# Fourth to seventh product of a Strassen-like down projection summed in PSUM, and a value projection's second weights and transposes moved behind its first units

## The chip, the cores and the metric

One core of one Trainium2 chip. The time is in device microseconds (us) for one execution of the whole kernel; smaller is better. Engines are named as in the profile: PE is TensorE (matmuls), PEld its weight loads, DVE is VectorE, ACT is ScalarE, POOL is GpSimd, SP is SyncE, whose queue issues every DMA here.

## The reference

One decoder layer on a sequence of 1024 tokens with 1024 features, all in float32. Three sub-layers, each with a residual, a gate and a LayerNorm:

```
def swiglu(h, w_gate, w_up, w_down):
    return (jax.nn.silu(h @ w_gate) * (h @ w_up)) @ w_down
...
h = modulate(x, sh1, sc1)
y = swiglu(h, ffn1_w_gate[l], ffn1_w_up[l], ffn1_w_down[l])
x = layer_norm(ALPHA * x + (1 + g1) * (MACARON * y), ln1_g[l], ln1_b[l])
h = modulate(x, sh2, sc2)
y = token_mix(h, w_in[l], b_forget[l], swa_sinks[l], grp_gain[l], w_out[l])
x = layer_norm(ALPHA * x + (1 + g2) * y, ln2_g[l], ln2_b[l])
h = modulate(x, sh3, sc3)
y = swiglu(h, ffn2_w_gate[l], ffn2_w_up[l], ffn2_w_down[l])
x = layer_norm(ALPHA * x + (1 + g3) * (MACARON * y), ln3_g[l], ln3_b[l])
```

The inner width of the two feed-forward parts is 2816. `token_mix` begins with one projection of h; its value columns and forget-gate columns (648 in all) are computed first, as "units" of 128 tokens.

## The kernel before

Every float32 operand is split into a high and a low part (`split`: ACT casts the high part on L102, DVE subtracts it on L103), and each product of two tiles is three matmuls (`mm3`, L106 to L108).

The two down projections, `down(0, ...)` and `down(1, ...)`, use Strassen's scheme in Winograd's form: the 1024x2816 by 2816x1024 product is cut in halves each way and done as seven half-size products instead of eight. A product is 11 steps (`NG`) of 12 matmuls 128x128x512, into four PSUM banks, one for each 128 tokens of the half. `DOWN` gives the order of the products and their operands: A11, A12, A22, S1 to S4 come from memory (`aT`, L412), B11 to B22 are tiles of the down weights (`home`, L383), and T1 to T4 are sums of these, made on DVE in `weight`: T2 costs three sums a step (L393, L395, L396), T1's step makes T3 (L400) and, in the second feed-forward part, multiplies B21 by the gate (L402).

A product's result leaves its banks while the next product runs in other banks (`PBANKS`: "tp tp y y" and "mm mm mm o" by turns). The running sums of the scheme stand in SBUF stashes (`x1`, `x2`, `x3`, `u4`): a first product is copied by ACT (L477), later ones are added by DVE (L479, L481, L483, L485, L486, L495). `add_to` puts a finished quarter of the output into the residual with two DVE instructions (L423, L424). Such work is held in a list `todo` whose entries are taken one by one behind the steps of the following products. For the last quarter the sum goes straight from the banks to the residual (L490 for the first feed-forward part, L491).

`tail` is the number of last steps of the seventh product that run bank by bank, so that the first banks are finished early: 2 in the first down projection, 7 in the second.

Tiles come from rings of slots: `h` (14 slots: weights, stashes, LayerNorm rows, some operands), `w` and `z` (operands), `u` (loads), `t` (sums), and PSUM `mm` 3, `o` 1, `y` 2, `tp` 2. The order on each engine and queue is fixed when the kernel is built, by a planner that takes whatever is ready by its own estimate of times, earlier code first; slots of a ring are handed out in the order of the code.

After the first down projection, the kernel loads and splits the weights of both value projections (`wv_load` twice, 8 tiles each: ACT L740, DVE L741), normalises the second half of the tokens (four norms, `ln_steps`, up to L170), and then runs 16 units: first-half tokens with `wva` (k = 0 to 3) and `wvb`, then second-half tokens with both. A unit is 24 matmuls into one bank of `mm`, evacuated by ACT (L761) and DVE (L762). Behind the first-half units stand the eight "chunks" that transpose the normalised second half (PE L185 into `tp`, ACT L186, then a split):

```
                if hf == 0:
                    if t or pz:
                        steps[3 + t + 4 * pz]()
```

The second down projection is followed by the last LayerNorm (`final_b`): statistics for four token blocks (`ln_stats`, L158 to L165), then for each block the affine steps (L1333 to L1339) and the store of the output (L1341, L1343).

Of the kernel before, what the change touches and what calls it, by code (L numbers as in the profile page):

```python
# [46 lines left out]
def layer_kernel(ctx, tc, xT, x, c, adaT, adab, wg1, wu1, wd1, wqk, wv1, wv2, bf, sinks,  # L47
# [57 lines left out]
    def mm3(o, lh, ll, rh, rl, start, stop):  # L105
        T.matmul(o, lh, rh, start=start, stop=False)  # L106
        T.matmul(o, lh, rl, start=False, stop=False)  # L107
        T.matmul(o, ll, rh, start=False, stop=stop)  # L108
# [46 lines left out]
    def ln_stats(src):  # L155

        s6 = small([P, 2, 6], "bn", 4)
        V.bn_stats(s6[:, 0], src[:, :HT])  # L158
        V.bn_stats(s6[:, 1], src[:, HT:])
        mv = small([P, 2], "mv", 4)  # L160
        V.bn_aggr(mv, s6)
        ve = small([P, 1], "ve", 4)
        V.tensor_scalar(ve, mv[:, 1:2], LN_EPS, None, op0=ALU.add)
        rs = small([P, 1], "rs", 4)
        G.tensor_tensor(rs, ve, nhalf[:, :1], ALU.pow)  # L165
        return mv, rs

    def ln_norm(src):
        mv, rs = ln_stats(src)
        V.tensor_scalar(src, src, mv[:, 0:1], rs, op0=ALU.subtract, op1=ALU.mult)  # L170
# [194 lines left out]
    def down(ai, wd, gate, alpha, load, steps_a, tail=TAIL):  # L365
# [4 lines left out]
        sums = {}  # L370
# [15 lines left out]

        def weight(kind, g):
            if kind in ("B11", "B21", "B22"):
                return home(kind, g)
            if kind == "T2":  # L390
                b12 = home("B12", g)
                b11, b21, b22 = (raw[k, 0, g] for k in ("B11", "B21", "B22"))
                V.tensor_tensor(b11, b12, b11, ALU.subtract)  # L393
                t = st("t", [P, HT])
                V.tensor_tensor(t, b22, b11, ALU.subtract)  # L395
                V.tensor_tensor(b21, t, b21, ALU.subtract)  # L396
                return t
            if kind == "T1":
                b12, b21 = raw["B12", 0, g], raw["B21", 0, g]
                V.tensor_tensor(b12, raw["B22", 0, g], b12, ALU.subtract)  # L400
                if ai:
                    V.tensor_tensor(b21, b21, gate[:, cols[0]], ALU.mult)  # L402
            return raw[{"T1": "B11", "T3": "B12", "T4": "B21"}[kind], 0, g]
# [13 lines left out]
        def stash():  # L417
            return st("h", [P, 4, HT])

        def add_to(xt, k, n, s, eng=V):  # L420

            y = xt[k][:, cols[n]]
            eng.tensor_tensor(s, s, gate[:, cols[n]], ALU.mult)  # L423
            V.scalar_tensor_tensor(y, y, alpha, s, op0=ALU.mult, op1=ALU.add)  # L424
# [16 lines left out]
        xs = []  # L441
        for i in range(7):
            banks = [psum(q) for q in PBANKS[2 if i == 6 and not ai else i % 2].split()]

            def mul(a, w, g, k):
                mm3(banks[k], a[:, 0, k * P:(k + 1) * P], a[:, 1, k * P:(k + 1) * P], w[:, 0], w[:, 1],
                    g == 0, g == NG - 1)

            tl = tail if i == 6 else 1
            for g in range(NG - tl):  # L450
                a, w = get(i, g)
                for k in range(4):
                    mul(a, w, g, k)
                if i in (0, 4) and 2 <= g < 6:
                    if g == 2:
                        xs.append([])
                    xs[-1].append(load(i // 4, g - 2))
                if todo:
                    for f in todo.pop(0):
                        f()  # L460
            aw = [get(i, g) for g in range(NG - tl, NG)]
            if i in (0, 1, 2, 4):
                new = stash()
                if i == 0:
                    x1 = new
                elif i == 1:
                    x2 = new
                elif i == 2:
                    x3 = new
                else:  # L470
                    u4 = new
            for k in range(4):
                for j in range(tl):
                    mul(*aw[j], NG - tl + j, k)
                b = banks[k]
                if i in (0, 2):
                    A.copy(new[:, k], b)  # L477
                elif i in (1, 4):
                    V.tensor_tensor(new[:, k], x1[:, k], b, ALU.add)  # L479
                    if i == 4:  # L480
                        V.tensor_tensor(x3[:, k], x3[:, k], b, ALU.add)  # L481
                elif i == 3:
                    V.tensor_tensor(x1[:, k], x1[:, k], b, ALU.add)  # L483
                elif i == 5:
                    V.tensor_tensor(u4[:, k], u4[:, k], b, ALU.add)  # L485
                    V.tensor_tensor(x1[:, k], x1[:, k], b, ALU.add)  # L486
                else:
                    s = xs[1][k][:, cols[0]]
                    if not ai:
                        V.tensor_tensor(b, b, gate[:, cols[0]], ALU.mult)  # L490
                    V.tensor_tensor(s, s, b, ALU.subtract)  # L491
            if i == 1:
                todo = [[lambda k=k: add_to(xs[0], k, 0, x2[:, k])] for k in range(4)]
# [11 lines left out]
        while todo:  # L505
            for f in todo.pop(0):
                f()
# [172 lines left out]
    def ln_steps(zt, hf, m, dst, split_to, park=None):  # L680

        def norm(k):
            ln_norm(zt[k])
# [37 lines left out]
    def steps1(z):  # L721
# [5 lines left out]
              steps1)  # L727
# [5 lines left out]
    def wv_load(src, ncol):  # L733
        r = []
        for d0, nk in ((0, 3), (3, 3), (6, 2)):
# [7 lines left out]
        return r  # L743
# [552 lines left out]
    def final_a(zt):  # L1296
# [3 lines left out]
        def stats(k):  # L1300
# [3 lines left out]
            s1, s2, nm, ve = (q[:, j:j + 1] for q in [small([P, 2, 6], "bn", 4)[:, 0]] for j in range(4))  # L1304
# [18 lines left out]
    def final_b(zt):  # L1323
# [20 lines left out]
        for k in range(4):  # L1344
            sc[k] = ln_stats(zt[k])
# [3 lines left out]
    final_b(down(1, wd2, gate_load(2), 1.0, load_x2, final_a, 7))  # L1349
# [59 lines left out]
```

## Time and profile before

| | us |
|---|---|
| median of 3 runs | 1815.85 (1813.96 to 1819.73) |
| the profiled execution, whole | 1817.26 |
| its span, first to last instruction | 1815.5 |
| PE busy | 1750.9 |
| DVE busy | 1547.4 |
| ACT busy | 764.8 |
| first down projection, from its first matmul | 447.40 |
| value projection's units | 661.03 to about 731 |
| second down projection, first to last matmul | 1583.02 to 1796.06 |

A row of the view by windows shows, for a stretch of the span, the busy time of each engine with its number of instructions, the granted clock of PE, the share of DMA and the bytes per second. A row of the timeline shows start, duration, engine, line, operation, output and input, and in brackets how long its engine had been idle and what ended that.

### The profile page before, as it was taken

What the parts mean: (1) busy time and instruction counts of PE and PEld (TensorE: products, weight loads), DVE (VectorE), ACT (ScalarE), POOL (GpSimd) and SP (SyncE); (2) the same over time, 40 slices, a digit from 0 to 9 for tenths busy, and PEclk for the clock granted to TensorE, in tenths of its full rate; (3) what the DMA queues carried; (4) which work ended last, traced back from release to release, by engine and by line L of the source; (5) the groups of instructions that cost most, each with busy time, mean ns of one, the idle gap of its engine ahead of it and who ended that gap; (6) DMA issues with size and microseconds to landing.
All of it is one profiled execution on the core that took longest, in us unless ns stands there. A gap on an engine that the chain in (4) does not pass through costs nothing.

```text
span 1815.5 us, 23554 instructions
## 1 busy us (share of the span) xinstructions
PE 1750.9 (96%) x8114; PEld 1439.7 (79%) x8114; DVE 1547.4 (85%) x2806; ACT 764.8 (42%) x1465; POOL 23.0 (1%) x32
## 2 busy tenths in 40 slices
PE   7999999999999989999999989899999999999995
PEld 5788888888888879877777768678888888888884
DVE  7999999999597996378878887998887878879999
ACT  5433333333544342376556641633233333344480
POOL 0000000000000000000000000000000000000000
PEclk9999999999999999999999999999999999999998
DMA  9355555547754335655677862333233232675442
GB/s 364 123 198 179 191 201 185 178 161 275 259 168 146 88 118 196 215 156 169 180 216 215 238 215 87 117 122 128 87 132 101 99 105 87 231 231 165 134 146 81
DMA packets 147048, 303.44 MB, mean 167 GB/s; under 512 B 15385, under 2 KB 29297, under 8 KB 146929
## 3 DMA queue, kind: packets, MB, share of 16 engines
q1 hardware_dynamic: 146928, 301.94, 51.7%
q8 instruction: 64, 1.05, 0.3%
q14 instruction: 56, 0.45, 0.1%
HBM read 224.17 MB, written 77.71 MB: 166 GB/s over the span
## 4 chain that ended last, share of the span: by engine, by line
PE 83%; DVE 10%; ACT 3%; DMA 2%; issue 1%; POOL 0%; SPq 0%; DVEq 0%; ACTq 0%; POOLq 0%
PE y L106 11%; PE y L107 11%; PE y L108 11%; PE mm L108 10%; PE mm L106 10%; PE mm L107 9%; PE o L106 3%; PE o L108 3%; PE o L107 3%; PE tp L108 2%; PE tp L107 2%; PE tp L106 2%; DVE h L103 1%; PE tp L1121 1%; PE o L1125 1%
## 5 line engine op out<-in xcount | busy, mean ns | idle before, releaser
L102 ACT CAST w<-u 128x512 fp32r<-128x512 f32 x303 | 186.5, 622 | 397.5 <-PE y L108 164.0
L106 PE MATMUL y<-h,w 128*128 128x512 f32 x728 | 287.3, 395 | 5.2 <-ACT h L102 2.1
L107 PE MATMUL y<-h,w 128*128 128x512 f32 x728 | 285.7, 392 | 0.0
L108 PE MATMUL y<-h,w 128*128 128x512 f32 x728 | 284.9, 392 | 0.0
L103 DVE TENSOR_TENSOR w<-u,w 128x512 fp32r<-128x512 f32 x303 | 206.9, 688 | 24.0 <-ACT w L102 23.3
L106 PE MATMUL mm<-h,w 128*128 128x512 f32 x528 | 207.1, 393 | 18.5 <-ACT h L102 15.4
L108 PE MATMUL mm<-h,w 128*128 128x512 f32 x528 | 207.1, 393 | 0.4 <-DVE w L103 0.4
L107 PE MATMUL mm<-h,w 128*128 128x512 f32 x528 | 207.1, 393 | 0.3 <-DVE h L103 0.2
L106 PEld LDWEIGHTS y<-h,w 128*128 128x128 f32 x728 | 137.0, 188 | 33.5 <-ACT h L102 2.5
L108 PEld LDWEIGHTS y<-h,w 128*128 128x128 f32 x728 | 136.8, 188 | 26.6
L107 PEld LDWEIGHTS y<-h,w 128*128 128x128 f32 x728 | 136.9, 188 | 25.9 <-DVE h L103 0.2
L102 ACT CAST w<-t 128x512 fp32r<-128x512 f32 x106 | 65.5, 621 | 185.2 <-PE mm L108 68.4
L106 PEld LDWEIGHTS mm<-h,w 128*128 128x128 f32 x528 | 99.9, 189 | 40.7 <-ACT h L102 15.8
L107 PEld LDWEIGHTS mm<-h,w 128*128 128x128 f32 x528 | 100.2, 190 | 22.1 <-DVE h L103 1.5
L108 PEld LDWEIGHTS mm<-h,w 128*128 128x128 f32 x528 | 100.1, 190 | 21.7 <-DVE w L103 1.1
L102 ACT CAST z<-u 128x512 fp32r<-128x512 f32 x88 | 54.5, 622 | 107.2 <-PE y L108 45.2
L103 DVE TENSOR_TENSOR z<-u,z 128x512 fp32r<-128x512 f32 x88 | 60.5, 692 | 37.3 <-ACT z L102 37.3
L103 DVE TENSOR_TENSOR t<-tp,t 128x512 fp32r<-128x512 f32 (+1 forms) x126 | 73.0, 586 | 20.8 <-ACT t L102 19.5
L102 ACT CAST w<-h 128x512 fp32r<-128x512 f32 x111 | 68.1, 616 | 28.8 <-PE o L108 10.5
L102 ACT CAST t<-tp 128x512 fp32r<-128x512 f32 (+1 forms) x126 | 62.1, 501 | 42.1 <-PE tp L1121 41.0
L103 DVE TENSOR_TENSOR w<-h,w 128x512 fp32r<-128x512 f32 x111 | 75.8, 690 | 1.3 <-ACT w L102 1.3
L103 DVE TENSOR_TENSOR w<-t,w 128x512 fp32r<-128x512 f32 x106 | 73.0, 691 | 1.6 <-ACT w L102 1.1
(357 smaller groups left out, 3941.8 us busy)
## 6 DMA issues: line engine op xcount, KB each, us to landing
u<-aT SPq DMA_DIRECT2D x154, 256.0 KB, 2.7
q<-in_adaT SPq DMA_DIRECT2D x56, 512.0 KB, 3.4
u<-in_wg SPq DMA_DIRECT2D x92, 256.0 KB, 3.0
u<-in_wu SPq DMA_DIRECT2D x90, 256.0 KB, 2.8
aT<-z SPq DMA_DIRECT2D x44, 512.0 KB, 3.5
h<-in_wd SPq DMA_DIRECT2D x88, 256.0 KB, 4.7
qkd<-w SPq DMA_DIRECT2D x26, 512.0 KB, 3.6
aT<-b SPq DMA_DIRECT2D x22, 512.0 KB, 4.1
```

Of the source, the lines that this page charges most:

```text
L102: A.copy(hi, src)
L103: V.tensor_tensor(lo, src, hi.bitcast(F32), ALU.subtract)
L106: T.matmul(o, lh, rh, start=start, stop=False)
L107: T.matmul(o, lh, rl, start=False, stop=False)
L108: T.matmul(o, ll, rh, start=False, stop=stop)
L1121: T.transpose(pt[:, tok(i - q0)], sps[i][:, tok(j)], ident)
L1125: T.matmul(po[:, c0:], vt, ph[:, c0:], start=j == 0, stop=False)
```

## The change

The order of the seven products becomes P1 (A11 B11), P2 (A12 B21), S2 T2, S1 T1, S4 B22, S3 T3, A22 T4. The third, fourth and fifth products are added by PE to the banks that hold the first one (no `start`); the seventh is added to the banks of the sixth, with T4's sign turned. DVE's adds out of the banks become ACT copies of the running sum (after the first, third and fourth product into `u`, `u` again and `u4`, and of the sixth into `p7`), and the second quarter goes from the banks straight into `add_to`. The weights B22 and B12 are asked for step by step from the seventh step of the first product on (`coming`, `AHEAD`). The gate of the last quarter is applied on the banks in both down projections, not on B21 in the second. `second` adds the sixth product, puts the fourth quarter into the residual, and begins that half's LayerNorm statistics (`ln_early`); all entries of `todo` are now taken before the last bank is done.

Ahead of the units only `wva` is loaded; `wvb`'s three pieces stand behind units 1 to 3, and the eight chunks stand two by two behind units 5 to 8. The first two units use banks of `y`.

```diff
-    DOWN = (("A11", "B11"), ("A12", "B21"), ("S4", "B22"), ("S2", "T2"), ("S1", "T1"), ("S3", "T3"), ("A22", "T4"))
-    PBANKS = ("tp tp y y", "mm mm mm o", "y y mm mm")
+    DOWN = (("A11", "B11"), ("A12", "B21"), ("S2", "T2"), ("S1", "T1"), ("S4", "B22"), ("S3", "T3"), ("A22", "T4"))
+    PBANKS = {0: "tp tp y y", 1: "mm mm mm o", 5: "mm mm mm o"}
+    AHEAD = 6
...
+    def ln_early(k, src):
+        begun_stats[k] = small([P, 2, 6], "bn2", 4)
+        V.bn_stats(begun_stats[k][:, 1], src[:, HT:])
...
+        coming = [(kind, g) for kind in ("B22", "B12") for g in range(NG)]
...
-                b12 = home("B12", g)
...
-                V.tensor_tensor(b21, t, b21, ALU.subtract)
+                V.tensor_tensor(b21, b21, t, ALU.subtract)
...
-                if ai:
-                    V.tensor_tensor(b21, b21, gate[:, cols[0]], ALU.mult)
...
+                if len(made) >= AHEAD and coming:
+                    home(*coming.pop(0))
                 made.append(operands(*DOWN[j], h, ring(j, h)))
...
+            if i in PBANKS:
+                sets[i in (1, 5)] = [psum(q) for q in PBANKS[i].split()]
+            banks = sets[i in (1, 5, 6)]
+            more = i not in PBANKS
...
-                    g == 0, g == NG - 1)
+                    g == 0 and not more, g == NG - 1, more)
...
                 if i in (0, 2):
-                    A.copy(new[:, k], b)
-                elif i in (1, 4):
-                    V.tensor_tensor(new[:, k], x1[:, k], b, ALU.add)
-                    if i == 4:
-                        V.tensor_tensor(x3[:, k], x3[:, k], b, ALU.add)
+                    A.copy(u[:, k], b)
+                elif i == 1:
+                    V.tensor_tensor(c[:, k], u[:, k], b, ALU.add)
                 elif i == 3:
-                    V.tensor_tensor(x1[:, k], x1[:, k], b, ALU.add)
+                    A.copy(u4[:, k], b)
                 elif i == 5:
-                    V.tensor_tensor(u4[:, k], u4[:, k], b, ALU.add)
-                    V.tensor_tensor(x1[:, k], x1[:, k], b, ALU.add)
-                else:
+                    A.copy(p7[:, k], b)
+                elif i == 6:
+                    for _ in range(3):
+                        pop()
                     s = xs[1][k][:, cols[0]]
-                    if not ai:
-                        V.tensor_tensor(b, b, gate[:, cols[0]], ALU.mult)
-                    V.tensor_tensor(s, s, b, ALU.subtract)
+                    V.tensor_tensor(b, b, gate[:, cols[0]], ALU.mult)
+                    V.tensor_tensor(s, s, b, ALU.add)
...
-            elif i == 3:
-                todo = [[lambda k=k: V.tensor_tensor(x3[:, k], x3[:, k], x1[:, k], ALU.add)] for k in range(4)]
             elif i == 4:
-                todo = [[lambda k=k: add_to(xs[0], k, 1, x3[:, k])] for k in range(4)] + steps_a(xs[0])
+                todo = [[lambda k=k, b=banks[k]: add_to(xs[0], k, 1, c[:, k], b)] for k in range(4)] + steps_a(xs[0])
             elif i == 5:
-                z = [[lambda k=k, n=n: add_to(xs[1], k, n, (x1, u4)[n][:, k], V)] for n in range(2) for k in range(4)]
+                def second(k):
+                    V.tensor_tensor(u4[:, k], u4[:, k], p7[:, k], ALU.add)
+                    add_to(xs[1], k, 1, u4[:, k])
+                    if early:
+                        early(k, xs[1][k])
+                z = [[lambda k=k: second(k)] for k in range(4)]
+                z += [[lambda k=k: add_to(xs[1], k, 0, u[:, k])] for k in range(4)]
...
-    wva = wv_load(wv1, NV1)
-    wvb = wv_load(wv2, NV2)
+    wva, load_a = wv_load(wv1, NV1)
+    wvb, load_b = wv_load(wv2, NV2)
+    run_all(load_a)
     steps = ln_steps(xb, 1, mod2, t_tile, h2_split(1))
     run_all(steps[:4])
+    between = [[f] for f in load_b] + [[]] + [steps[4 + 2 * k:6 + 2 * k] for k in range(4)]
...
-                p = psum("mm")
+                p = psum("y" if hf + pz == 0 and k < 2 else "mm")
...
-                    if t or pz:
-                        steps[3 + t + 4 * pz]()
-                    if t == 3 and pz:
-                        steps[11]()
+                    run_all(between.pop(0))
```

More of the change, by code (lines that the diff above doesn't have):

```diff
@@ L103, in split, with mm3 @@
         V.tensor_tensor(lo, src, hi.bitcast(F32), ALU.subtract)
[L105 to L108, printed above, removed]
+    def mm3(o, lh, ll, rh, rl, start, stop, more=False):
+        T.matmul(o, lh, rh, start=start, stop=False, skip_group_check=more)
+        T.matmul(o, lh, rl, start=False, stop=False, skip_group_check=more)
+        T.matmul(o, ll, rh, start=False, stop=stop, skip_group_check=more)
     def halves(t):
@@ L369, in down @@
         mixed = {}
-        sums = {}
         def home(kind, g):
@@ L441, in down, with pop @@
         xs = []
+        sets = {}
+        def pop():
+            if todo:
+                for f in todo.pop(0):
+                    f()
         for i in range(7):
-            banks = [psum(q) for q in PBANKS[2 if i == 6 and not ai else i % 2].split()]
+            if i in PBANKS:
+                sets[i in (1, 5)] = [psum(q) for q in PBANKS[i].split()]
+            banks = sets[i in (1, 5, 6)]
+            more = i not in PBANKS
             def mul(a, w, g, k):
                 mm3(banks[k], a[:, 0, k * P:(k + 1) * P], a[:, 1, k * P:(k + 1) * P], w[:, 0], w[:, 1],
-                    g == 0, g == NG - 1)
+                    g == 0 and not more, g == NG - 1, more)
             tl = tail if i == 6 else 1
@@ L505, in down @@
         while todo:
-            for f in todo.pop(0):
-                f()
+            pop()
         return xs[1]
```

68 lines of the change are left out of this document (33 added, 35 removed).

## The prediction

> **What bounds the kernel now.** I read the page first (shares and chain), then the products of the second down projection as windows, then the gap after the first one, then the end.
>
> ```profile
> span 1815.5 us, 23554 instructions
> ...
> PE 1750.9 (96%) x8114; PEld 1439.7 (79%) x8114; DVE 1547.4 (85%) x2806; ACT 764.8 (42%) x1465; POOL 23.0 (1%) x32
> ...
> PE 83%; DVE 10%; ACT 3%; DMA 2%; issue 1%; POOL 0%; SPq 0%; DVEq 0%; ACTq 0%; POOLq 0%
> ```
>
> TensorE ends most of the chain. Fewer VectorE instructions pay only where PE waits. The windows of the second down projection, one for each product, and a last one for what follows PE:
>
> ```profile
> 1583.02:1614.21 31.19, 30.22 (x134) 24.70 (x132) 28.74 (x42) 14.43 (x25) 0.00 (x0) 1.00 0.78 263
> 1614.21:1644.13 29.92, 29.92 (x134) 24.78 (x132) 15.41 (x25) 13.16 (x24) 0.00 (x0) 1.00 0.57 174
> 1644.13:1674.05 29.92, 29.92 (x134) 24.77 (x132) 29.92 (x51) 14.24 (x25) 0.00 (x0) 1.00 0.54 161
> 1674.05:1703.97 29.92, 29.92 (x134) 24.78 (x132) 29.92 (x50) 12.82 (x23) 0.00 (x0) 1.00 0.54 164
> 1703.97:1734.21 30.24, 30.23 (x134) 24.70 (x132) 29.53 (x44) 13.95 (x25) 0.00 (x0) 1.00 0.41 123
> 1734.21:1764.13 29.92, 29.92 (x134) 24.78 (x132) 27.84 (x58) 26.36 (x48) 3.19 (x4) 1.00 0.50 148
> 1764.13:1796.06 31.93, 30.44 (x133) 24.47 (x131) 31.73 (x53) 7.25 (x14) 0.00 (x0) 1.00 0.22 75
> 1796.06:1815.50 19.44, 0.00 (x1) 0.00 (x0) 15.91 (x36) 2.44 (x3) 2.93 (x4) 0.61 0.26 108
> ```
>
> The first column after the bounds is the length, then PE, PEld, DVE, ACT. A product takes 29.92 us with PE never idle, although DVE (29.92 of 29.92) is full in the third and fourth. So most of the 20 DVE instructions that the first down projection loses, and the 27 of the second, lie under PE and give nothing by themselves. Lost are 1.3 us in the first product, 0.3 in the fifth, 2.0 in the seventh, and 19.44 us behind PE's end in which DVE works 15.91.
>
> The other place is the start of the units, in windows of 5 us:
>
> ```profile
> 660.00:665.00 5.00, 5.00 (x34) 4.80 (x33) 5.00 (x11) 0.27 (x1) 0.00 (x0) 1.00 0.31 89
> 665.00:670.00 5.00, 5.00 (x36) 5.00 (x36) 3.99 (x9) 3.29 (x7) 0.00 (x0) 1.00 0.72 229
> 670.00:675.00 5.00, 2.16 (x14) 1.68 (x13) 4.58 (x12) 2.25 (x6) 1.07 (x2) 1.00 0.88 274
> 675.00:680.00 5.00, 2.25 (x9) 1.83 (x10) 4.48 (x11) 0.00 (x0) 1.12 (x3) 0.72 0.36 127
> 680.00:685.00 5.00, 5.00 (x24) 4.95 (x23) 4.25 (x7) 2.06 (x3) 0.00 (x0) 0.60 0.59 183
> 685.00:690.00 5.00, 5.00 (x37) 4.99 (x36) 4.37 (x7) 2.03 (x4) 0.00 (x0) 1.00 0.44 161
> ```
>
> Three windows hold 14 + 9 + 24 = 47 PE instructions where 36 each would be 108. The 61 missing ones are 61 x 5/36 = 8.5 us: 5.6 us of waits (next fence), the rest mostly the granted clock at 0.72 and 0.60.
>
> **The change, step by step.**
>
> *The units.* The first matmul of a unit, PE's waits (total, times, longest) and DVE in the same stretch:
>
> ```profile
> 661.03 0.30 PE L106 MATMUL mm<-h,h 128*128 128x320 f32 x1
> ```
>
> ```profile
> PE tp L185 <- DVE z L170: 5.6, 3, 2.9
> ```
>
> ```profile
> 668.27 1.87 DVE L741 TENSOR_TENSOR h<-u,h 128x328 fp32r<-128x328 f32 x4 [1.01 <-ACT h L740]
> ...
> 673.10 0.50 DVE L741 TENSOR_TENSOR h<-u,h 128x328 fp32r<-128x328 f32 x1 [0.35 <-ACT h L740]
> ...
> 678.17 0.44 DVE L762 TENSOR_TENSOR w<-mm,w 128x320 fp32r<-128x320 f32 x1
> ...
> 679.40 0.81 DVE L170 TENSOR_SCALAR z<-z,s_mv,s_rs 128x1024 f32<-128x1024 f32 x1 [0.33 <-POOL s_rs L165]
> ```
>
> The transposes stand in PE's order behind three units and wait for the norms (L170, the fourth at 679.40); DVE has `wvb`'s splits among the norms, and the first evacuation (L762) comes only at 678.17, so the three `mm` banks are full too. After: five units find a bank (two `y`, three `mm`), and the transposes stand behind the fifth. A unit is 24 x 5/36 = 3.3 to 3.5 us, so the fifth starts at about 675 and the transposes come at about 678.5. DVE's norms lose `wvb`'s 8 splits (1.87/4 = 0.47 each, 3.7 us) and four statistics of 0.6 (2.4 us), so the fourth norm is done near 680.2 - 6.1 = 674. `wvb` is needed from 675 to 678; its last split was at 673.10, and its loads wait for the same slots of `u` as before. Margins of 2 to 5 us: 8.5 us go, between 4 (one of the waits comes back) and 8.5. I take 7.5.
>
> *The end.* Six rows of the timeline, DVE, PE, POOL and SP:
>
> ```profile
> 1788.56 1.31 DVE L423 TENSOR_TENSOR h<-h,b 128x512 f32<-128x512 f32 x2
> ...
> 1795.57 0.68 DVE L424 SCALAR_TENSOR_TENSOR z<-z,h 128x512 f32<-128x512 f32 x1
> ...
> 1810.56 1.41 DVE L1339 SCALAR_TENSOR_TENSOR z<-z,s_rs,h 128x512 f32<-128x512 f32 x2
> ```
>
> ```profile
> 1795.67 0.39 PE L108 MATMUL y<-h 128*128 128x512 f32 x1
> ```
>
> ```profile
> 1798.92 0.55 POOL L165 TENSOR_TENSOR s_rs<-s_ve,nhalf 128x1 f32<-128x1 f32 x1 [39.92 <-DVE s_ve L163]
> ```
>
> ```profile
> 1811.33 0.99 SPq L1341 DMA_DIRECT2D out<-z x2
> ```
>
> The last quarter's `add_to` runs from 1788.56 to 1795.57, the statistics and affine steps to 1811.97, and 3.5 us more pass to the span's end. The easy reading is that eight `add_to` and four statistics leave the tail. But DVE is full throughout (27.84, 31.73 and 15.91 us in the last three windows), so moving work ahead of PE's end only pushes other work behind it. What counts is how much DVE has left to do from 1734 on. In 29.92 us it does 50 or 51 instructions, 0.60 us each. From 1734 the change takes away the rest of the fifth product's adds (3 still to come) and the sixth's 8, and adds 4 in `second` and 4 gates: 3 fewer, 1.8 us. The 24 fewer before 1734 (14.4 us) leave DVE idle in the fourth and fifth products, which it can use only to split ahead, as far as slots go: from about 1.5 steps of lead to about 4, 5 instructions, 3.0 us. The lead now is read from the splits of the sixth product's first and third step, against PE's start of it at 1734.21:
>
> ```profile
> 1729.12 0.71 DVE L103 TENSOR_TENSOR h<-u,h 128x512 fp32r<-128x512 f32 x1
> ...
> 1737.73 0.69 DVE L103 TENSOR_TENSOR h<-u,h 128x512 fp32r<-128x512 f32 x1
> ```
>
> Together 4.8 us. The bounds: 1.8 (no lead), and everything done but the last block's chain: gate, add, one statistics (0.6 each), POOL's 0.55 with small steps (1.3), four affine steps (2.7) and 0.3 of latency make 6.1 us behind PE, where now DVE ends 1811.97 - 1796.06 = 15.9 behind: 9.8 us.
>
> *T2 one product earlier.* This is what speaks against. The third product's steps now need 5 DVE instructions (3.0 us) against PE's 29.92/11 = 2.72, and in its first part stand also the second product's 4 adds and 8 of `add_to`: 67 in all, 40.2 us for 29.92. Before, T2 stood in the fourth product and ran ahead in the third.
>
> ```profile
> 1640.63 1.85 SPq L383 DMA_DIRECT2D h<-in_wd x4
> ...
> 1671.18 1.85 SPq L383 DMA_DIRECT2D h<-in_wd x4
> ```
>
> ```profile
> h<-in_wd SPq DMA_DIRECT2D x88, 256.0 KB, 4.7
> ```
>
> T2 needs B22 and B12. Their loads (4.7 us) left at 1640 and 1671 because their slots stand behind the stashes of the second and third product. After the change they stand behind the first product's stash alone, so twelve loads leave near 1615 and are there by about 1625. DVE is idle for 14.5 us of the second product, 24 instructions, 8 triples of T2. By 1644 I expect 5 or 6, and 4 steps split ahead (8). That leaves 67 - 8 - 16 = 43, 25.8 us for 29.92. Cost 0 to 8.5 us in each down projection; I take 0.5 each, since DVE was as full in the same place before and PE did not wait.
>
> *Loads of B22 in the first product.* Up to 8 more of 256 KB before its stash, 2.1 MB at the 263 GB/s of that window: 8 us of traffic where DMA is at 0.78. Operands are loaded 4 steps (11 us) ahead. 0 to 2 us, I take 0.5; the 1.3 us already lost there stay.
>
> *Copies in the path.* The third, fourth and fifth products write the same banks, so do the sixth and seventh; each of six hand-overs now waits for ACT. The nearest row is the third product's copy in the first down projection:
>
> ```profile
> 535.55 0.59 ACT L477 COPY h<-tp 128x512 f32<-128x512 f32 x1
> 536.03 0.62 ACT L102 CAST h<-h 128x512 fp32r<-128x512 f32 x1
> ```
>
> ```profile
> 535.12 0.39 PE L108 MATMUL tp<-w,z 128*128 128x512 f32 x1
> ...
> 537.39 0.39 PE L106 MATMUL mm<-w,z 128*128 128x512 f32 x1
> ```
>
> The copy starts 0.04 us after bank 0's last matmul and ends at 536.14, 1.25 us before the next product starts. One ACT instruction in between is covered, two are not: 0 to 1 us each, I take 0.5 for all. The Trainium skill, "PSUM — Partial Sum Buffer", in its summary of rules, says to read PSUM from another bank than the one matmuls are writing, which is what the old turns did and the new order gives up. By that rule every hand-over would cost up to 1 us and the sum would be 5.5 us worse; the trace's 1.25 us of margin speaks for less.
>
> *The rest.* Twenty-odd fewer DVE adds, 8 more ACT copies in each down projection (ACT works 13 to 14 of 29.92 us in most products) and the gate on 4 tiles in place of 11 lie under PE: nothing, until DVE or ACT is the later one.
>
> **Sum.** 1817.26 - 7.5 - 4.8 + 1.0 + 0.5 + 0.5 = 1807.0 for the profiled execution. That execution lies 1.41 above the median of 1815.85, so 1805.5 as a median. A measurement of this kernel tells about 0.3% (5.4 us) from no change.
>
> **The rivals.** *T2 crowds PE out.* If the planner puts fewer than about 4 triples of T2 ahead of the third product, DVE there needs more than 29.92 us and PE waits, up to 8.5 us in each down projection. For: 67 instructions where 50 fit. Against: the 14.5 idle us just before. It costs 17 against gains of 12.3: 1817.26 - 12.3 + 1.0 + 17 = 1823, as a median 1821.5, slower.
>
> *DVE gets free before PE ends.* If the lead grows beyond the slots I count, the tail shrinks by its full 9.8 and the seventh product's wait goes too:
>
> ```profile
> PE tp L107 <- DVE h L103: 1.5, 1, 1.5
> ```
>
> 1817.26 - 7.5 - 9.8 - 1.5 + 2 = 1800.5, median 1799. For: DVE loses 14.4 us ahead of 1734. Against: the slots, and ACT at 26.36 us in the sixth product.
>
> *The waits only move.* PE waits for `wvb` at the fifth unit, or transposes are planned too early again, half the gap stays, and the lead gives nothing: 1817.26 - 4 - 1.8 + 2 = 1813.5, median 1812, no measurable change. The Trainium skill, "TensorE: Matmul & The Clock Gate" ("What's actually happening"), has the clock halved after an idle window of about 3.4 us; by it a remaining wait of 3 us would cost no slow stretch and this case would be 1.5 us better. The trace differs in size: three waits, the longest 2.9 us, close together, were enough for 0.60.
>
> **How the numbers follow.** The forecast 0.51, free DVE 0.20, waits that move 0.18, crowding 0.11. The first two give faster, 0.71; the third same, 0.18; the last slower, 0.11. The forecast's own range is 1800 to 1811. To hold 8 in 10 it goes down to 1796 (8.5 + 11.3 us gained and no new wait) and up to 1816, into the moved waits with 4 us of copies or crowding.
>
> **What would show it.** Right: no PE wait on L170, 36 PE instructions in each 5 us from 661 to 690 and a clock of 1.00 there; the third product at 29.92 us with DVE busier than before in the second; DVE's last affine step about 11 us behind PE's last matmul. Wrong: a third product above 30.5 us, PE idle on an ACT copy at a product's first matmul, or PE waiting for the split of `wvb`.

## The result, and the profile after

The changed kernel takes 1800.06 us (median of 4 runs, 1798.39 to 1802.0) against 1815.91 (4 runs, 1813.96 to 1819.73): a ratio of 0.9911, 95% interval 0.9891 to 0.993, or 16 us less (13 to 20). The profiled execution takes 1802.0, 15.26 less than the one before. One run of an experiment below (e9_u_late, 1954.07 us) had a granted clock of 0.847, where all others had 0.987 to 0.996, and is left out of its ratio. The page of the changed kernel, its span, its busy times and the shares of the chain:

```profile
span 1800.2 us, 23514 instructions
...
PE 1749.5 (97%) x8114; PEld 1439.8 (80%) x8114; DVE 1520.0 (84%) x2759; ACT 772.3 (43%) x1481; POOL 23.1 (1%) x32
...
PE 80%; DVE 11%; ACT 3%; DMA 3%; issue 2%; POOL 0%; SPq 0%; ACTq 0%; DVEq 0%; POOLq 0%
```

47 VectorE instructions have gone and PE is about as busy as before (1749.5 us against 1750.9). The same windows as before, one for each product of the second down projection and one for what follows PE:

```profile
1576.89:1607.50 30.61, 30.22 (x134) 24.71 (x132) 24.54 (x35) 14.44 (x25) 0.00 (x0) 1.00 0.89 306
1607.50:1637.42 29.92, 29.92 (x134) 24.78 (x132) 28.91 (x48) 13.97 (x25) 0.00 (x0) 1.00 0.65 215
1637.42:1667.34 29.92, 29.92 (x134) 24.78 (x132) 29.92 (x51) 13.81 (x25) 0.00 (x0) 1.00 0.34 99
1667.34:1697.26 29.92, 29.92 (x134) 24.78 (x132) 18.90 (x29) 13.45 (x25) 0.00 (x0) 1.00 0.51 143
1697.26:1727.18 29.92, 29.92 (x134) 24.78 (x132) 27.77 (x42) 16.39 (x30) 0.00 (x0) 1.00 0.59 181
1727.18:1757.10 29.92, 29.92 (x134) 24.78 (x132) 25.18 (x53) 24.61 (x43) 2.58 (x4) 1.00 0.39 130
1757.10:1788.17 31.07, 30.42 (x133) 24.49 (x131) 29.69 (x57) 10.62 (x20) 1.79 (x2) 1.00 0.15 51
1788.17:1800.20 12.03, 0.00 (x0) 0.00 (x0) 8.45 (x16) 0.81 (x1) 1.79 (x2) 0.72 0.36 143
```

The second to sixth products take 29.92 us, with T2 now in the third: DVE does 28.91 us of work in the second product, where it did 15.41. The last row is 12.03 in place of 19.44. The units, in the windows of 5 us in which PE had waited or run at a lowered clock:

```profile
670.00:675.00 5.00, 5.00 (x36) 5.00 (x35) 4.58 (x11) 1.26 (x3) 0.39 (x1) 1.00 0.59 167
675.00:680.00 5.00, 5.00 (x38) 4.99 (x37) 5.00 (x6) 1.55 (x4) 0.00 (x0) 1.00 1.04 352
680.00:685.00 5.00, 5.00 (x38) 5.00 (x37) 5.00 (x8) 3.03 (x6) 0.00 (x0) 1.00 1.02 344
```

Here 14, 9 and 24 instructions became 36, 38 and 38, at a clock of 1.00. The end, in the timelines of DVE and PE:

```profile
1775.65 0.68 DVE L103 TENSOR_TENSOR h<-h,h 128x512 fp32r<-128x512 f32 x1
1777.33 0.70 DVE L505 TENSOR_TENSOR mm<-mm,b 128x512 f32<-128x512 f32 x1 [0.99 <-PE mm L109]
...
1795.93 0.75 DVE L1358 SCALAR_TENSOR_TENSOR z<-z,s_rs,h 128x512 f32<-128x512 f32 x1
```

```profile
1787.78 0.39 PE L109 MATMUL o<-h 128*128 128x512 f32 x1
```

The last split ends 11.84 us before PE (7.39 in the kernel before), DVE then idles for 0.99 us until the first bank is done, and its last step ends at 1796.68, 8.5 us behind PE instead of 15.9.

The difference by stages, from the two profiled executions: units 70.71 to 61.73 us (-9.0); from the next projection to the second down projection, called the middle stage below, 851.28 to 854.15 (+2.9); PE in the second down projection 213.04 to 211.28 (-1.8); PE's end to the span's end 19.44 to 12.03 (-7.4). Together -15.3.

The +2.9 stands in a stage that the change does not touch, but for two rings of small LayerNorm tiles that have 2 slots in place of 4, so I looked for it first. Two of PE's waits there and the granted clock in windows of 2 us, changed kernel:

```profile
989.76 0.44 PE L1145 MATMUL o<-t,h 128*128 128x384 f32 x1 [1.47 <-DVE t L103]
992.19 0.77 PE L1115 MATMUL mm<-q,q 128*128 128x512 f32 x1 [0.97 <-DVE s_mneg L1118]
```

```profile
990.00:992.00 2.00, 1.21 (x7) 0.83 (x6) 1.50 (x8) 0.89 (x4) 0.14 (x1) 0.84 1.02 401
992.00:994.00 2.00, 1.81 (x5) 1.48 (x6) 1.50 (x5) 1.30 (x4) 0.00 (x0) 0.50 1.12 257
994.00:996.00 2.00, 2.00 (x10) 1.81 (x9) 1.70 (x3) 1.27 (x3) 0.00 (x0) 0.50 0.70 227
996.00:998.00 2.00, 2.00 (x7) 1.51 (x6) 2.00 (x4) 1.11 (x3) 0.00 (x0) 0.50 0.99 228
998.00:1000.00 2.00, 2.00 (x11) 1.69 (x10) 2.00 (x5) 0.78 (x2) 0.00 (x0) 0.95 1.04 219
```

The same place in one of the experiments below (e2_down, the same code here):

```profile
990.22 0.44 PE L1144 MATMUL o<-t,h 128*128 128x384 f32 x1 [1.33 <-DVE t L103]
992.73 0.47 PE L1114 MATMUL mm<-q,q 128*128 128x512 f32 x1 [1.05 <-DVE s_mneg L1117]
```

```profile
991.00:993.00 2.00, 0.94 (x5) 0.64 (x4) 1.42 (x6) 0.89 (x5) 0.00 (x0) 1.00 1.16 363
993.00:995.00 2.00, 2.00 (x13) 1.63 (x12) 1.85 (x4) 1.82 (x6) 0.00 (x0) 1.00 1.02 266
```

The waits are alike, 2.4 us in both; the clock is halved behind them in one execution and not in the other. Laid side by side matmul by matmul, the changed kernel loses 2.4 us to e2_down between 992.75 and 997.87, and another 2.3 around 1072 and 1185, where its clock is lowered longer. Over the 14 kernels profiled here this stage takes from 848.5 to 854.4 us, and its code is the same. Added up over its windows of 2 us, each 2 us x (1 - granted clock), the lowered clock took 10.2 us of it in the changed kernel's execution, 5.1 in the one before and 3.4 in e2_down's. So the +2.9 is put down to the execution and not to the change, and differences of 3 us in the total are told from the traces by stage, not from the medians.

### The profile page after: what moved, and what is told of

Read it like the earlier page. It is cut to its first block, busy times and chain, and to the rows that moved or that the text cites. A ratio compares the mean times of both kernels' runs of the same rounds, so it can differ in the third digit from the quotient of the medians.

```text
span 1800.2 us, 23514 instructions
## 1 busy us (share of the span) xinstructions
PE 1749.5 (97%) x8114; PEld 1439.8 (80%) x8114; DVE 1520.0 (84%) x2759; ACT 772.3 (43%) x1481; POOL 23.1 (1%) x32
## 4 chain that ended last, share of the span: by engine, by line
PE 80%; DVE 11%; ACT 3%; DMA 3%; issue 2%; POOL 0%; SPq 0%; ACTq 0%; DVEq 0%; POOLq 0%
PE y L107 11%; PE y L108 11%; PE y L109 11%; PE mm L107 9%; PE mm L109 9%; PE mm L108 9%; PE o L107 3%; PE o L108 3%; PE o L109 3%; DVE h L103 2%; PE tp L107 2%; PE tp L109 2%; PE tp L108 2%; DVE w L103 1%; PE tp L1140 1%
## 5 line engine op out<-in xcount | busy, mean ns | idle before, releaser
L107 PEld LDWEIGHTS mm<-h,w 128*128 128x128 f32 x528 | 99.8, 189 | 40.7 <-ACT h L102 15.9
```

Source lines behind the costliest of these rows:

```text
L107: T.matmul(o, lh, rh, start=start, stop=False, skip_group_check=more)
```

## The experiments

Stages of each profiled execution, in us, and the ratio to the kernel before with its interval:

| kernel | units | middle | PE, 2nd down | DVE end behind PE | ratio |
|---|---|---|---|---|---|
| before | 70.71 | 851.28 | 213.04 | 15.91 | |
| after | 61.73 | 854.15 | 211.28 | 8.51 | 0.9911 (0.9891 to 0.993) |
| e1_units | 62.68 | 854.37 | 213.16 | 15.91 | 0.9967 (0.9956 to 0.9979) |
| e2_down | 63.07 | 848.53 | 212.19 | 8.53 | 0.9906 (0.9893 to 0.9919) |
| e3_no_early | 61.74 | 849.09 | 212.62 | 7.41 | 0.9887 (0.9874 to 0.9899) |
| e4_last_adds | 61.75 | 851.90 | 212.24 | 10.64 | 0.9909 (0.9897 to 0.9921) |
| e5_more_dve | 61.75 | 849.57 | 212.50 | 8.51 | 0.991 (0.9895 to 0.9925) |
| u1_mm_banks | 61.73 | 850.51 | 211.81 | 8.51 | 0.9909 (0.9894 to 0.9924) |
| u2_wvb_first | 61.74 | 850.30 | 212.08 | 8.51 | 0.9909 (0.9892 to 0.9925) |
| u3_transposes_early | 63.16 | 853.19 | 212.37 | 8.51 | 0.9922 (0.9907 to 0.9936) |
| e9_u_late | 61.75 | 852.01 | 211.56 | 11.88 | 0.9926 (0.9913 to 0.994) |
| e8_need | 61.75 | 851.93 | 211.35 | 8.51 | 0.9912 (0.9896 to 0.9927) |
| e11_old_units_no_early | 63.04 | 853.15 | 212.27 | 7.42 | 0.991 (0.9896 to 0.9924) |
| e12_none_early | 61.75 | 852.26 | 212.85 | 7.41 | 0.9903 (0.9889 to 0.9917) |

"Units" is the first unit's first matmul to the next projection's; "middle" ends at the second down projection's first matmul.

**The two parts alone.** e1_units: the kernel before with the new units part.

```diff
-    wva = wv_load(wv1, NV1)
-    wvb = wv_load(wv2, NV2)
+    wva, load_a = wv_load(wv1, NV1)
+    wvb, load_b = wv_load(wv2, NV2)
+    run_all(load_a)
...
-                p = psum("mm")
+                p = psum("y" if hf + pz == 0 and k < 2 else "mm")
```

> The kernel before with the units part of the change alone (wvb's pieces behind units 1 to 3, transposes behind units 5 to 8, two banks of y); the down projections are the old ones. Theory: the units gain by themselves what the changed kernel gains there, so the first matmul of the next projection comes at about 722.7 instead of 731.7 (-9.0 us), the second down projection stays as it was (213.0 us, 19.4 us behind PE's end), and the time is 1807 if nothing is given back, 1810 if the attention stage gives 3 us back as in the changed kernel's profile. Rival: part of the 9.0 us is owed to the first down projection (four statistics, 2.4 us of VectorE, are begun there); then the gap closes by 6 to 7 us only and the time is about 1809 to 1812.

e2_down: the changed kernel with these lines as they were before.

> The changed kernel with the old units part (both value weights loaded ahead, transposes one by one behind units 2 to 8, all units in banks of mm). Theory: the two parts add up; the second down projection and the end give 1.8 + 7.4 = 9.2 us, the units nothing, 1806.7. Rival: VectorE's relief in the first down projection (20 instructions, 4 statistics begun) shortens the gap of the units too, 1802 to 1805.

The units part alone closes most of the gap (62.68 us, 8.0 of 9.0). So does the down part alone, with the old loads, banks and transposes (63.07, 7.6). PE's waits between 661 and 723 us in e2_down:

```profile
PE tp L195 <- DVE z L180: 0.4, 1, 0.4
```

The last split of wvb and the last norm in e2_down:

```profile
667.72 0.50 DVE L759 TENSOR_TENSOR h<-u,h 128x328 fp32r<-128x328 f32 x1 [0.43 <-ACT h L758]
...
673.85 0.81 DVE L180 TENSOR_SCALAR z<-z,s_mv,s_rs 128x1024 f32<-128x1024 f32 x1 [0.33 <-POOL s_rs L175]
```

Both came about 5.5 us later in the kernel before (673.10 and 679.40). The first down projection no longer fills VectorE at its end (from 600 to 661 us it works 51.4 us in e2_down, 59.7 in the kernel before), the value weights are split earlier, and the norms meet the transposes in time. The two parts are two cures of one wait: by the ratios they save 6.0 us (e1_units, 0.33% of 1817) and 17.1 (e2_down), 23 together, and the whole change 16.2; the 7 us too many, uncertain by some us as the intervals are, are about the size of the gap, counted twice. For e1_units the theory had the unchanged end right, and the gap closed by 8.0 us, between its 9.0 and the rival's 6 to 7; the time of 1812.14 lies just above both expectations, in a session in which the kernel before took 1818.52 and with a middle stage of 854.37 in the profile. For e2_down the rival was right: the down projection shortens the gap too.

e11_old_units_no_early asks what in the first down projection does it: the begun statistics or the fewer adds.

```diff
-              steps1, early=ln_early)
+              steps1)
...
-    final_b(down(1, wd2, gate_load(2), 1.0, load_x2, final_a, 7, ln_early))
+    final_b(down(1, wd2, gate_load(2), 1.0, load_x2, final_a, 7))
```

(with the old units part as in e2_down)

> The changed kernel with the old units part and without begun statistics in either down projection. With them and the old units part the gap at the units was closed but for 0.4 us (fourth norm at 673.9). Theory A: four statistics of 0.6 us were what brought the norms in time; without them the fourth norm comes at about 676 and PE waits 2 to 4 us again at the transposes, next projection at 726 to 729. Theory B: the 20 fewer adds of the first down projection do it (value weights split ahead of the units' start); the fourth norm stays below 675 and the projection starts within 1.5 us of 724.3. The end behind PE is 7.4 us as without begun statistics; 1798 to 1804.

63.04 us: theory B's time, though the fourth norm came at 676.16, as theory A had it. The first transposes need only the first norms, and PE waited for them once, 0.3 us. The statistics were not needed here; the rest of the new down projection suffices. That it is the fewer adds is likely, and was not told apart from its other edits.

**Inside the units part**, one thing undone at a time (the changed kernel otherwise).

```diff
-                p = psum("y" if hf + pz == 0 and k < 2 else "mm")
+                p = psum("mm")
```

> The changed kernel with all units in the three banks of mm. Theory: the fourth unit finds a bank only when the first is evacuated; if VectorE evacuates promptly now that wvb's splits are gone from among the norms, the two y banks are worth 0 to 1 us. Rival (as the prediction counted, five units must find a bank): 3 of the 9 us come back at the first matmul of the next projection, 1803.

```diff
-    run_all(load_a)
+    run_all(load_a + load_b)
-    between = [[f] for f in load_b] + [[]] + [steps[4 + 2 * k:6 + 2 * k] for k in range(4)]
+    between = [[]] * 4 + [steps[4 + 2 * k:6 + 2 * k] for k in range(4)]
```

> The changed kernel with wvb loaded and split ahead of the norms, as before; transposes behind units 5 to 8 and the y banks stay. Theory: the transposes behind the fifth unit give the norms time enough, the splits (8 of 0.47 us) lie under PE, 0 to 1 us lost. Rival: the norms, 3.7 us later, meet the transposes at 678.7 and PE waits 1 to 4 us there, with a clock below 1.00 behind it.

```diff
-    between = [[f] for f in load_b] + [[]] + [steps[4 + 2 * k:6 + 2 * k] for k in range(4)]
+    old = [[]] + [[f] for f in steps[4:10]] + [steps[10:]]
+    between = [a + b for a, b in zip([[f] for f in load_b] + [[]] * 5, old)]
```

> The changed kernel with the transposes one by one behind units 2 to 8, as before; wvb's pieces stay behind units 1 to 3, the y banks stay. Theory: the place of the transposes in the order is what makes the gap, most of the 9 us comes back, 1807 to 1809. Rival: with VectorE free of wvb's splits the norms are done when the transposes come, 1800 to 1802.

The banks and the late wvb are worth nothing here (61.73 and 61.74 us); the place of the transposes is worth 1.4 us (63.16). With the new down projection as cover none of the three is needed for most of the gap. Which of them closes it in e1_units, under the old down projection, was not tried.

**The end: what made it short?** e5_more_dve gives VectorE its work back under the fourth and fifth product:

```diff
             split(a[:, 0], a[:, 1], r)
+            if ai and an in ("S1", "S4"):
+                V.tensor_tensor(a[:, 1], r, a[:, 0].bitcast(F32), ALU.subtract)
```

> The changed kernel, but in the second down projection each step of the fourth and fifth product (S1 and S4) does the subtraction of its first operand's split twice: 22 more VectorE instructions, 13.2 us, ahead of the sixth product. Theory (VectorE's relief before the sixth product makes the lead, and the lead makes the short end): the fourth and fifth product have 11.0 + 2.2 us idle, all of it is filled, the splits come later, the wait in the seventh product grows from 0.7 to 1.5 or more and the end by 2 to 6 us, 1802 to 1807. Rival (the end is short because eight adds and four statistics were moved ahead of the last banks; the relief lies under PE): within 0.5 of the changed kernel.

The fourth and fifth product, and from the sixth to the span's end, in e5_more_dve:

```profile
1663.45:1693.37 29.92, 29.92 (x134) 24.78 (x133) 26.66 (x43) 13.46 (x25) 0.00 (x0) 1.00 0.49 153
1693.37:1723.29 29.92, 29.92 (x134) 24.78 (x133) 29.92 (x45) 16.18 (x30) 0.00 (x0) 1.00 0.43 130
1723.29:1797.00 73.71, 60.31 (x265) 49.27 (x263) 66.36 (x128) 36.12 (x63) 6.47 (x8) 0.95 0.34 118
```

Of the 13.2 us of idle time 3.3 are left (26.66 and 29.92 of 29.92), and the end stayed at 8.51. The wait in the seventh product was 1.37 in place of 0.65, but in e2_down, which has the changed kernel's down projection, it was 1.41, so this is no effect of the edit that can be told. The rival was right: free VectorE time under PE, by itself, did not make the end short. The lead was hardly tested: from the sixth product on there are 5 instructions more than in the changed kernel (128 against 123), only 2 of them splits, and the last split ends 11.81 us before PE, as there (11.84). The same stretch, sixth product to the end, first in the kernel before and then in the changed one:

```profile
1734.21:1815.50 81.29, 60.36 (x265) 49.25 (x263) 75.48 (x145) 36.05 (x63) 6.12 (x8) 0.91 0.34 110
```

```profile
1727.18:1800.20 73.02, 60.34 (x265) 49.27 (x263) 63.31 (x123) 36.03 (x63) 6.17 (x8) 0.95 0.29 98
```

22 instructions and 12.2 us less. Counted by kind in the timelines, by what begins in the stretch: 13 adds out of banks gone, 7 splits fewer, 10 instructions of `add_to` fewer, 4 adds of `second` and 4 gates more. Eight of the ten are the third quarter's `add_to` out of `u`, complete since the third product; the first and last of their four second halves in the changed kernel:

```profile
1702.03 0.68 DVE L433 SCALAR_TENSOR_TENSOR z<-z,h 128x512 f32<-128x512 f32 x1
...
1714.48 0.68 DVE L433 SCALAR_TENSOR_TENSOR z<-z,h 128x512 f32<-128x512 f32 x1
```

They run in the fifth product (their gate products in the fourth, at 1669.64 to 1673.86), though the code has them behind the sixth. e9_u_late takes this away, with no instruction added:

```diff
-                z += [[lambda k=k: add_to(xs[1], k, 0, u[:, k])] for k in range(4)]
+                z += [[lambda k=k: add_to(xs[1], k, 0, *((p7[:, k], u[:, k]) if ai else (u[:, k],)))] for k in range(4)]
```

> The changed kernel, but in the second down projection the gate product of the third quarter (u, complete since the third product) is written into the tile of p7, so that its four add_to can't start before the sixth product is done, as in the kernel before; no instruction is added. Theory: the changed kernel needs 22 fewer VectorE instructions from the sixth product on than the kernel before (121 against 143), and 8 of them are these add_to, pulled into VectorE's idle time of the fourth to sixth product because u is complete early. Put back, 4.8 us of VectorE's work come behind the sixth product: last split later by up to 4.8 us, the end behind PE 8.5 + 2 to 4.8 us, PE's wait in the seventh product above 1.5 us; 1802 to 1806. Rival: the short end comes from the banks being finished one by one and from the order of the code; the eight find room in the seventh product (0.99 us idle) and before, 1800 to 1801.

The last window of e9_u_late, sixth product to the span's end, and the first of the four moved adds:

```profile
1725.14:1801.20 76.06, 60.40 (x265) 49.29 (x263) 67.84 (x131) 35.79 (x63) 5.11 (x8) 0.91 0.30 107
```

```profile
1775.03 1.30 DVE L433 SCALAR_TENSOR_TENSOR z<-z,h 128x512 f32<-128x512 f32 x2
```

Exactly 8 instructions more (131 against 123), all eight of them now behind the last split, which starts at 1773.22, and the end is 11.88 in place of 8.51: 3.4 us, as the theory had it. The way there was another: the last split comes no later (11.90 us before PE's end, 11.84 in the changed kernel), and PE's wait in the seventh product did not grow (0.27). The ratio moves to 0.9926, the way the trace does, but within the intervals.

e4_last_adds keeps them early-ready and changes only the order of the code:

```diff
-                    for _ in range(3):
-                        pop()
                     s = xs[1][k][:, cols[0]]
```

> The changed kernel, but in the second down projection the last four add_to (8 instructions) are written behind the last banks as in the kernel before, not taken ahead of each bank. Theory A (the order of the code makes the short end): up to 8 x 0.6 = 4.8 us come back behind the first bank, 1803 to 1805. Theory B (VectorE's work before decides, the planner fills its idle time with whatever is ready): the adds are ready before the first bank is done and go ahead of it anyway, 1800 to 1801.

10.64: 2.1 us come back, between the theories. Four gate products went ahead, their four adds (4 x 0.6 = 2.4) did not. They could not: each writes the same tile `z` as the add out of the bank, which in this order of the code stands before it. In the timeline the add out of the first bank starts at 1776.22 and the first of the four at 1777.45. So for these adds the order of the code does count, through the tile they share.

e3_no_early leaves out the begun statistics of the second down projection (the second of the two edits of e11).

> The changed kernel, but in the second down projection the last LayerNorm's statistics are not begun early: four instructions of 0.6 us go back behind the last banks. Theory A: VectorE now has caught up before the first of the last banks is done (idle 0.99 us at 1777.33) and works without a gap from there to the end, so what is moved back behind that point costs its full time, +2.4 us, 1802.5. Theory B (the prediction's accounting, VectorE full throughout): the four only change places with splits, 1800 within 0.5.

Both theories missed: the end got shorter. The splits that the four statistics had been pushing back come earlier, and so does the first bank (VectorE begins on it 13.1 us before PE's end, 10.8 in the changed kernel). DVE in e3_no_early:

```profile
1769.02 0.68 DVE L103 TENSOR_TENSOR h<-h,h 128x512 fp32r<-128x512 f32 x1
1769.62 1.28 DVE L168 BATCH_NORM_STATS2 s_bn<-z 128x6 f32<-128x512 f32 x2
1770.82 0.68 DVE L505 TENSOR_TENSOR mm<-mm,b 128x512 f32<-128x512 f32 x1
```

The last split ends 14.18 us before PE's end (1783.88) in place of 11.84, two statistics fill the time in which DVE had idled, and the end is 7.41, 1.1 us less; e11 and e12 show the same 7.42 and 7.41. e12_none_early drops them in the first down projection as well.

> The changed kernel without begun statistics in either down projection. In the second one, leaving them out made the end 1.1 us shorter behind PE and the time 1797.5. Theory: the new units part has 2 to 4 us of room (fourth norm at 670.4, transposes at 678.7), so 2.4 us later statistics cost nothing there, next projection at 722 to 723, time as with the second one's left out, 1797 to 1799. Rival: the first down projection needs them, PE waits 1 to 3 us at the transposes, 1799 to 1801.

Its units take the same 61.75 us. The median was 1797.46 for e3_no_early and 1799.96 for e12_none_early, whose traces differ by 3.2 us in the untouched middle stage. Beginning the statistics early costs 1.1 us at the end; that a kernel without it is faster as a whole is likely by the traces and not settled by the ratios.

**T2's loads.** e8_need loads B22 and B12 where T2 needs them.

```diff
-                if len(made) >= AHEAD and coming:
-                    home(*coming.pop(0))
...
+            if kind == "T2":
+                home("B22", g)
+                home("B12", g)
```

> The changed kernel in which B22 and B12 are loaded at the step of T2 that needs them, not step by step from the first product's seventh step on. Theory (loads ahead let T2 run ahead in the second product, where VectorE works 28.91 us): loaded at need they still leave the queue as soon as slots are free, the third product stays at 29.92 us or loses 0 to 3 us in each down projection, 1800 to 1806. Rival (the prediction's crowding): T2's 33 instructions fall into the third product, PE waits up to 8.5 us in each, up to 1817.

PE's waits in the first down projection of e8_need, and none like them in the second; then the third product there:

```profile
PE tp L108 <- DVE w L103: 1.0, 2, 0.6
PE tp L107 <- ACT w L102: 0.3, 1, 0.3
```

```profile
507.59:539.76 32.17, 30.94 (x133) 24.46 (x132) 32.06 (x54) 14.15 (x26) 0.00 (x0) 1.00 0.51 170
```

The first unit starts at 663.34 in place of 661.01: the loads ahead are worth 2.3 us in the first down projection and nothing in the second. The third product takes 32.17 us with VectorE full: this is the crowding that the prediction feared, of 2.3 us and not of 8.5.

## Why the prediction was right in sign and wrong in its sizes

The forecast was 1805.5 in a range of 1796 to 1816; 1800.06 was measured, at the lower edge of the forecast's own 1800 to 1811. Faster was right, 5 us too little. In part that it is no further off is luck: in the profiled executions the stages that the change touches gave 18.2 us where 10.3 were forecast, and the untouched middle stage took 2.9 of them back.

*The units, -7.5 forecast, -9.0 found.* The end of the gap is as described: no wait on the norms, 36 to 38 instructions in each window, clock 1.00. The bound of 8.5 came from counting missing instructions and was a little low; windows of 2 us of the kernel before show the lowered clock:

```profile
676.00:678.00 2.00, 0.36 (x2) 0.12 (x2) 1.87 (x4) 0.00 (x0) 0.55 (x1) 0.80 0.25 96
678.00:680.00 2.00, 1.81 (x7) 1.63 (x8) 1.67 (x6) 0.00 (x0) 0.55 (x1) 0.50 0.19 59
680.00:682.00 2.00, 2.00 (x10) 1.96 (x9) 1.74 (x3) 0.32 (x1) 0.00 (x0) 0.50 0.96 284
682.00:684.00 2.00, 2.00 (x9) 2.00 (x8) 1.51 (x3) 1.75 (x3) 0.00 (x0) 0.50 0.46 149
```

PE worked 0.36, 1.81, 2.00 and 2.00 us of these windows, at half the clock, and so lost about 3.1 us; with 5.6 us of waits this makes 8.7 of the 9.0. The step that failed is the credit. I named both wvb's splits and the down projection's relief as helping the norms, but put all of it under the units part; e2_down shows that the down projection alone closes 7.6 us of the gap, e1_units that the units part alone closes 8.0.

*The end, -4.8 forecast, -7.4 found; the mis-sized term.* The argument that moved work only pushes other work behind it held for the statistics: e3_no_early shows it. That what counts is all of VectorE's work from the sixth product on did not hold: e5_more_dve has 3.05 us more of it (66.36 against 63.31) and the same end. The count failed too. I had 3 instructions fewer (11 adds out of banks gone, 8 instructions new) and 5 splits' worth of lead, 4.8 us; there were 22 fewer, 12.2 us: 13 adds gone and 8 instructions new, 7 splits, and 10 instructions of `add_to`, which the sum put at nothing. The failing step is the sentence that DVE can use its idle time in the fourth and fifth products "only to split ahead". `u` is complete since the third product, so the planner put eight instructions of `add_to` there; without that e9_u_late loses 3.4 us. What is left then, 15.91 - 11.88 = 4.0 us, is close to the 4.8 of the two terms that the sum did have; how it divides between them, no run shows. Of the 12.2 us only part reached the end: DVE now has idle time in the sixth and seventh products and waits 0.99 us for a bank. DVE's last step ends 8.5 us behind PE, where the sign of being right was about 11.

*T2 and the loads of B22, +1.5 forecast, nothing found.* The second down projection became 1.8 us shorter, in part by chance: PE's wait in the first product fell from 0.97 to 0.39 and in the seventh from 1.49 to 0.65, but e2_down and u1 to u3, with the same down projection, take 211.81 to 212.37, 0.7 to 1.2 us less than the kernel before. T2 ran ahead in the second product, 8 of its 11 triples begun where 5 or 6 were counted on; the first and the last of the 8 by their second sums in the timeline of the changed kernel:

```profile
1614.27 0.69 DVE L407 TENSOR_TENSOR t<-h,h 128x512 f32<-128x512 f32 x1
...
1636.54 0.69 DVE L407 TENSOR_TENSOR t<-h,h 128x512 f32<-128x512 f32 x1
```

The crowding rival is refuted for these loads (the third product takes 29.92 us in both down projections); e8_need shows the load order to matter by 2.3 us.

*The copies, +0.5 forecast, none found.* No product starts late on an ACT copy: the windows of the second to the sixth product are all 29.92, and the seventh follows without a gap. The tightest hand-over found in the second down projection is that of the sixth product's third bank: ACT's copy of it ends at 1757.69, and the seventh product first writes it at 1758.46, 0.77 us later. The prediction also worked out 5.5 us from the Trainium skill's rule to read PSUM from another bank than the one being written ("PSUM — Partial Sum Buffer", summary of rules). They did not come, and the case does not test the rule: the banks are handed over one by one, and none is read while it is written.

*The rivals.* Free DVE before PE's end came nearest in time (1799), and half by its mechanism: DVE even idles, and the last split comes 4.5 us earlier against PE's end; but 3.4 of the 7.4 us came from ready work and not from lead (e9_u_late). For the rest lead is neither shown nor refuted, since e5_more_dve took little of it away. Moved waits: in the changed kernel not seen; in e1_units PE waits 0.3 us for a split of `wvb`.

## What to carry to other kernels

When a formula is rewritten, look not only for which instructions vanish but for which results become final earlier: work that depends on them can move under another engine by itself. Two edits that each remove the same wait do not add up; time each alone before a gain is credited. Work begun early on an engine that is full delays what the bottleneck is waiting for: the begun statistics cost 1.1 us at the end.

## What the hardware showed

The same two waits in the middle stage, 2.4 us in all, were followed by a halved clock in one execution and by a full one in another. By the rows above (0.84, then three at 0.50, then 0.95), the halved stretch is (0.16 + 3 x 0.50 + 0.05) x 2 / 0.5 = 6.84 us long, and the four windows of the kernel before give 3.4 x 2 = 6.8 us too.

The Trainium skill, "TensorE: Matmul & The Clock Gate" ("What's actually happening"), describes a free-running activity window of 3413 ns, whose phase differs from run to run. The traces agree. In the changed kernel the stretches of lowered clock before PE's end start at 991.36, 1069.87, 1168.86 and 1185.92, which are 23, 29 and 5 times 3.413 us apart. All 41 such stretches of the 14 profiles, from 60 us on, start on one grid of this kind in each profile, and last one or two windows; the grid's place differs between profiles (in e3_no_early a stretch starts at 989.71).

The same section has the clock halved after at least one idle window. Here the traces do not agree: no wait at that place is longer than 1.47 us. The window of the grid ahead of the halved clock in the changed kernel, and the same window in e2_down, where the clock stayed full:

```profile
987.95:991.36 3.41, 1.79 (x10) 1.17 (x8) 2.91 (x8) 1.13 (x4) 2.19 (x1) 1.00 0.78 310
```

```profile
987.95:991.36 3.41, 2.08 (x12) 1.47 (x11) 3.10 (x7) 1.64 (x5) 2.61 (x1) 1.00 0.96 269
```

PE worked 1.79 of 3.41 us in the first and 2.08 in the second. Over the 14 profiles, from 60 us on, a full clock was halved behind every window of the grid with less than 1.5 us of PE's work, and behind none with more than 1.83. So waiting for about half a window was enough, in one piece or in several. In these two profiles the grid lies alike; in e2_down the waits come 0.5 us later, and so one window holds less of them. Why windows with 1.5 to 1.83 us of work went either way is open.

The middle stage varied by 5.8 us over the 14 profiles. The lowered clock took 3.4 to 10.2 us of it, 1.7 for each window. Without it the stage still takes from 843.5 to 848.1 us; that remainder is open.
